# Hybrid attention and gating block: where the splits of the branch weights stand beside z, and where the last raw gate rows lie

## The chip, the core and the metric

One core of a Trainium2 chip. The metric is the device time of one execution in microseconds (us), the median of three runs. Engines: PE (TensorE, matrix products), DVE (VectorE), ACT (ScalarE), POOL (GpSimd) and SP (SyncE, which here issues most DMAs). Each takes its own queue of instructions in order and waits on semaphores.

## The reference

A decoder block on 2048 tokens of width 1024, in float32:

```python
h = _rmsnorm(x, norm_pre_mix[layer])
proj = jnp.einsum('bsd,de->bse', h, w_in[layer])   # q, k, v, u, z, two gates
y_attn = _mixer_dilated_attention(q, k, v)
y_gmlp = _mixer_chunked_gmlp(u, z, ...)
merged = (gate_a * jnp.einsum('bse,ed->bsd', y_attn, w_branch_attn[layer])
          + gate_b * jnp.einsum('bse,ed->bsd', y_gmlp, w_branch_gmlp[layer]))
y = jnp.einsum('bsd,de->bse', merged, w_out[layer])
```

Then a residual, a norm and a squared-ReLU MLP. The attention has three groups of dilated windows; their outputs are combined by a softmax over the groups' log-denominators. u and z go through Gelu, z through a layer norm and a product along the sequence.

## The kernel before

Every float32 matrix product is made of three products of rounded parts: each operand is split into a high part (`hi`, rounded) and the rest (`lo`, a subtraction), and PE runs hi x hi, hi x lo and lo x hi, lines 95 to 97. The helper `split` (line 67) writes the high part on ACT (line 70) or POOL (line 72) and subtracts on DVE or POOL (line 78). `split_in` (line 87) loads a raw row by an SP DMA (line 91) and splits it.

The sequence is cut into four chunks of 512 tokens. Work stands in a generator, `filler` (line 758), which is advanced in steps by other parts of the program: `u`, `z` of chunks 2 and 3, the gate products of `gates` (line 662), and last z of chunks 0 and 1. PE's order is the order in which the program writes it; the order on DVE, ACT, POOL and SP is made by a scheduler, where nothing else is said. `behind()` (line 175) ties what is written under it behind the latest instruction written for each engine, so that the scheduler puts it no earlier.

**Gates.** The gate and u columns are made by seven products each (a scheme of sums of blocks). `seq` lists them with half, operation i and pair n; `LAST` is the place in `seq` of the last ten products. `piece(t)` (line 613) loads the raw weights of product t by an SP DMA (line 627) into a small row `r` of a ring, `split_piece(t)` (line 630) splits it on POOL into one of the `spots`; `PIECES = 4` and `SPLITS = 3` say how many products ahead. The rows are four rows `gr` in two tiles, then `ga11`, `ga9`, `ga10` and two of the tiles that hold results (`zs[8:]`, called ga7 and ga8). Results go to DRAM by SP (line 714) one product later, and one or two entries of `ins` (the loads of the weights of z, `w_z`, and of the activations, `hT_b`) follow each product (line 717).

**z of chunks 0 and 1.** Each chunk has four tiles of 128 tokens; a tile is eight steps of three products (line 95 to 97), so 64 steps. After a tile ACT makes Gelu (line 572) and DVE statistics (lines 574 and 575); after four tiles DVE normalizes (line 579). The raw activations of chunk 1 (`hT_b`, line 1077) are loaded in the first eight steps.

**The combination of attention** (`combine`, line 953) for one chunk is a generator of five pieces: three loads of the groups' outputs into `cw` (line 958); maxima, differences, exponential, normalizers (lines 961 to 974); scaling on ACT (line 979, sixteen small instructions) and DVE (line 982, two); two additions (lines 984 and 985); eight transposes on PE (line 990) whose results ACT copies (line 993) and stores (line 994). Two chunks (2 and 3) are combined during the gates with tiles of their own. Chunks 0 and 1 use one place `cw`, one after the other, during z. The dictionary `todo` (line 1073) says behind which step of z a piece is written (2 stands for chunk 0, 3 for chunk 1):

```python
    todo = {12: (2,), 14: (2,), 17: (2,), 24: (2, 3), 38: (3,), 40: (3,), 43: (3,), 52: (3,)}
    for n in range(1, 54):
        steps(1)
```

**The branch weights** are six rows wb0 to wb5. `load_wb` (line 1063) loads a row into one of two raw rows and splits it, the high part on POOL, the rest on DVE; it is called at every sixth step. Its DMA, its copy on POOL and its subtraction on DVE are placed by the scheduler.

Behind z stands the merge: six rows `yt` are loaded (line 91, from `load_y`) and split on POOL, the gates are loaded (lines 1129 and 1138), opened by a sigmoid on ACT (line 1147), and the products with `wb` and `yt` are multiplied with them on DVE (line 1164).

Of the kernel before, what the change touches and what calls it, by code (L numbers as in the profile page):

```python
# [8 lines left out]
F32 = mybir.dt.float32  # L9
# [7 lines left out]
P = 128  # L17
S = 2048
D = 1024
# [22 lines left out]
def block_kernel(ctx, tc, a, out):  # L42
# [44 lines left out]
    def split_in(w, src, raw=None, hi_eng="pool", lo_eng="dve"):  # L87

        if raw is None:
            raw = f32(w)[:, 1]  # L90
        sp.dma_start(raw, src)
        split(w[:, 0], w[:, 1], raw, hi_eng, lo_eng)
# [82 lines left out]
    def behind():  # L175

        es, t = ExitStack(), mybir.EngineType
        for e in (t.Activation, t.DVE, t.Pool, t.SP):
            es.enter_context(tc.issue_after(next(i for i in reversed(nc.cur_bb.bb.instructions) if i.engine == e)))
        return es  # L180
# [432 lines left out]
    def piece(t):  # L613

        if t >= len(seq):
            return
        half, i, n = seq[t]
        raws = g_["raws"]
        r = raws[t % 4] if t < 8 else raws[4 + (t - LAST - 4) % 5] if t >= LAST + 4 else raws[(t - 8) % 5]
        if i < 3:  # L620
            src = w_src(w_at(n), i - 1)[:, :, :P]
        elif i == 5:
            src = s1g_d[n]
        else:
            kk, m = {6: (0, 0), 7: (0, 1), 3: (1, 0), 4: (1, 1)}[i]
            src = sg_d[n][:, kk, :, m * P:(m + 1) * P]
        sp.dma_start(r.rearrange("p (k c) -> p k c", k=4), src)
        g_["raw"][t] = r
# [33 lines left out]
    def gates():  # L662

        bank, todo, out_, ins = {}, [], [], []
        slots = [None, hp.tile([P, 2, 2, 4, 512], F32R, name="opB", tag="hT", bufs=2)]
        zs = wp.tile([P, 8, 512], F32, name="gz", tag="w", bufs=3)
        zs = [zs[:, n] for n in range(8)]
        xs = [st.tile([P, 512], F32, name=f"gx{n}", tag="ev", bufs=3) for n in range(3)]
        g_["b"].update({(1, 1): hT[2][:, :, :4], (1, 2): hT[2][:, :, 4:]})
        phases = [(half, ops) for half in (1, 0) for ops in PHASES]  # L670
        starts, t = {}, 0
        for n, (half, ops) in enumerate(phases):
            starts[t] = n
            t += PAIRS[half] * len(ops)
        for t, (half, i, n) in enumerate(seq):
            if t in starts:
                ph, t0 = starts[t], t
                if ph + 1 < len(phases):
                    s = (ph + 1) % 2
                    if not slots[s]:  # L680
                        slots[s] = hp.tile([P, 2, 2, 4, 512], F32R, name="opA", tag="hT", bufs=2)
                    for j, i2 in enumerate(phases[ph + 1][1]):
                        new = operand(phases[ph + 1][0], i2, slots[s][:, j])
                        ins += new[0]
                        todo += new[1]
                else:
                    ws, hs = want(5), reload_h(0)
                    ins += ws[:2] + hs[:4] + ws[2:] + hs[4:]
            elif todo and (t - t0) % 3 == 1 and t > t0 + 1:
                w, k = todo.pop(0)  # L690
                with behind():
                    split(w[:, 0, k:k + 2], w[:, 1, k:k + 2], f32(w)[:, 1, k:k + 2], "act", "pool")
            piece(t + PIECES)
            split_piece(t + SPLITS)
            if i in (1, 6, 5, 4):
                bank[n] = psum_mm(f"g{half}{i}{n}")
            p, w, h = bank[n], g_["w"].pop(t), g_["b"][half, i]
            for k in range(4):
                for m, (l, r) in enumerate(((0, 0), (0, 1), (1, 0))):
                    pe.matmul(p, w[:, l, k], h[:, r, k], start=i in (1, 6, 5, 4) and not k and not m,  # L700
                              stop=k == 3 and m == 2, skip_group_check=True)
                if (t, k) == (3, 2) and late:
                    sz_out(*late.pop(0))
                yield
            if t == 3:
                a = [ga.tile([P, 512], F32, name=f"ga{n_}", tag=f"ga{n_}", bufs=1) for n_ in range(12)]
                xs += a[:7]
                zs += a[7:9]
                vs = a[9:11]
                g_["vs"] = vs + xs[8:] + zs[8:]  # L710
                g_["raws"] += a[11:] + vs + zs[8:]
            x, z, fn = xs[n], zs[n], AF.Copy if n < 8 else AF.Gelu_apprx_tanh
            while out_:
                sp.dma_start(*out_.pop())
            for _ in range(2 if half and i == 4 or t in (LAST + 1, LAST + 2) else 1):
                if ins:
                    sp.dma_start(*ins.pop(0))
            if i == 1:
                act.activation(x, p, AF.Copy)
            elif i == 2:  # L720
                act.activation(z, p, fn)
                o = z, 0, 0
            elif i == 6:
                dve.tensor_add(z, x, p)
            elif i == 7:
                dve.tensor_add(x, x, p)
            elif i == 5:
                if (half, n) == (0, 0):
                    g_["vs"] = a[9:11]
                v = g_["vs"].pop(0)  # L730
                g_["vs"].append(v)
                dve.tensor_add(v, x, p)
                o = v, 1, 1
            elif i == 3:
                dve.tensor_add(z, z, p)
                o = z, 0, 1
            else:
                dve.tensor_add(x, x, p)
                o = x, 1, 0
            if n > 7 and i in (5, 3, 4):  # L740
                act.activation(o[0], o[0], fn)
            if i in (2, 5, 3, 4):
                c, dst = 2 * half + o[2], gate_d if n < 8 else u_d
                out_.append((dst[n % 8 * 2 + o[1], :, c * 512:(c + 1) * 512], o[0]))
        sp.dma_start(*out_.pop())
        yield
# [312 lines left out]
    e2r = ExitStack()  # L1059
    wbp = stack(e2r, "wbp", 1, side="right")  # L1060
    wb = [wbp.tile([P, 2, D], F32R, name=f"wb{k}") for k in range(6)]

    def load_wb(k):
        raw = wp.tile([P, D], F32, name=f"wbraw{k}", tag="raw", bufs=2)
        split_in(wb[k], a["w_branch"][:, k, :], raw)

    ez = ExitStack()
    zps[0] = stack(ez, "zp0", 1, side="right")
# [1 line left out]
    next(sg)  # L1070
    while not cw:
        steps(1)
    todo = {12: (2,), 14: (2,), 17: (2,), 24: (2, 3), 38: (3,), 40: (3,), 43: (3,), 52: (3,)}
    for n in range(1, 54):
        steps(1)
        if zin:
            sp.dma_start(*zin.pop(0))
        if n % 6 == 0 and n <= 36:
            load_wb(n // 6 - 1)
        if n == 48:  # L1080
            next(sg)
        for k in todo.get(n, ()):
            combined((0, k))
# [969 lines left out]
```

## Time and profile before

| | us |
|---|---|
| Median of three runs | 2675.07 (2674.3 to 2677.39) |
| The profiled execution, its time | 2677.99 |
| The profiled execution, its span | 2676.0 |
| PE busy | 2617.2 (98%) |
| DVE busy | 1652.9 (62%) |
| POOL busy | 1197.9 (45%) |
| ACT busy | 1087.0 (41%) |

The span goes from the first to the last instruction of the program on the core; the time holds what lies around it, 1.99 us here. The mean granted clock of PE is 0.993. Times inside the trace are counted from the span's start. In rows of a timeline stand the start, the length, the engine, the line, the operation, what is written <- what is read, sizes and count, and in brackets the idle time of the engine before it and who ended it. Buffer numbers are left out of names, so wb0 to wb5 all read wb. "yt" names both the combination's transposes on line 990 and the merge's rows on lines 72 and 78.

### The profile page before, as it was taken

Reading aid. Unit: us, or ns where it says so; the run is one execution under the profiler, and the core shown is the slowest. Engines: PE = TensorE matmul, PEld = TensorE weight load, DVE = VectorE, ACT = ScalarE, POOL = GpSimd, SP = SyncE. Lnnn points to the kernel's source line nnn. Section 1 sums busy time; section 2 is a strip of 40 time slices with the busy share of each in tenths; the row PEclk is TensorE's granted clock in tenths of the full one; section 3 lists DMA queues with packets and bytes.
Section 4 is the critical chain, followed back from the end, with each engine's and each line's share of the span. In section 5 each row is a group of like instructions: output and inputs, shape, how many; then the busy total and the mean of one; then the engine's idle time right before and its main releaser. Section 6 shows DMA issues by size and latency. Waiting matters only on the chain. (4 is left out here: it accounts for less than half of the span.)

```text
span 2676.0 us, 35501 instructions
## 1 busy us (share of the span) xinstructions
PE 2617.2 (98%) x12458; PEld 2185.3 (82%) x12458; DVE 1652.9 (62%) x2793; ACT 1087.0 (41%) x2278; POOL 1197.9 (45%) x1089
## 2 busy tenths in 40 slices
PE   9999999999999996999999999999999999999998
PEld 8888888888888884788878888888888888888887
DVE  5676665535434453765677655655437888888866
ACT  5213111254455432444445555655545333233334
POOL 0363354274464662310233564223315776676645
PEclk9999999999999998999999999999999999999999
DMA  8779768888888898543667464654343212222235
GB/s 320 280 248 319 261 229 292 291 281 251 291 281 243 236 303 301 203 168 134 200 231 262 130 218 159 209 154 129 106 145 119 87 56 87 87 87 87 87 109 214
DMA packets 389284, 528.29 MB, mean 197 GB/s; under 512 B 57009, under 2 KB 242097, under 8 KB 387570
## 3 DMA queue, kind: packets, MB, share of 16 engines
q1 hardware_dynamic: 300336, 436.03, 49.6%
q0 software_dynamic: 14992, 51.65, 5.1%
q10 hardware_dynamic: 73778, 38.35, 4.7%
q8 instruction: 98, 1.61, 0.3%
q14 instruction: 80, 0.66, 0.1%
HBM read 342.77 MB, written 183.17 MB: 197 GB/s over the span
## 5 line engine op out<-in xcount | busy, mean ns | idle before, releaser
L1904 PE MATMUL ya<-T_spots,s 128*128 128x512 f32 x1176 | 289.3, 389 | 1.0 <-ACT T_spots L70 0.6
L70 ACT ACTIVATE s<-sraw 128x768 fp32r<-128x768 f32 (+1 forms) x184 | 127.2, 696 | 330.3 <-POOL sraw L1705 156.2
L1904 PEld LDWEIGHTS ya<-T_spots,s 128*128 128x128 f32 x1176 | 220.6, 188 | 47.6 <-ACT T_spots L70 0.9
L78 DVE TENSOR_TENSOR s<-sraw,s 128x512 fp32r<-128x512 f32 x172 | 184.5, 1097 | 8.5 <-ACT s L70 7.2
L1377 PE MATMUL aa<-B,A 128*128 128x512 f32 x768 | 182.4, 390 | 1.4 <-ACT xs L1391 0.7
L1348 POOL TENSOR_TENSOR s<-w1r 128x512 f32<-128x512 f32 x32 | 42.4, 1324 | 307.7 <-DVE S L78 261.0
L700 PE MATMUL g<-opA,spots 128*128 128x512 f32 x672 | 170.0, 397 | 0.0
L1377 PEld LDWEIGHTS aa<-B,A 128*128 128x128 f32 x768 | 143.9, 188 | 31.9 <-ACT xs L1391 1.1
L700 PE MATMUL g<-opB,spots 128*128 128x512 f32 x648 | 164.5, 398 | 1.3 <-POOL spots L72 0.7
L1904 PE MATMUL yc<-T_spots,s 128*128 128x512 f32 x624 | 159.6, 389 | 0.0
L95 PE MATMUL x<-hT_a,wq 128*128 128x512 f32 x384 | 149.7, 390 | 0.0
L97 PE MATMUL x<-hT_a,wq 128*128 128x512 f32 x384 | 149.4, 389 | 0.0
L96 PE MATMUL x<-hT_a,wq 128*128 128x512 f32 x384 | 149.4, 389 | 0.0
L700 PEld LDWEIGHTS g<-opA,spots 128*128 128x128 f32 x672 | 121.2, 188 | 21.8
L78 POOL TENSOR_TENSOR spots<-gr,spots 128x512 fp32r<-128x512 f32 x98 | 127.7, 1307 | 22.3 <-PE g L700 8.3
L1904 PEld LDWEIGHTS yc<-T_spots,s 128*128 128x128 f32 x624 | 117.2, 188 | 24.3
L700 PEld LDWEIGHTS g<-opB,spots 128*128 128x128 f32 x648 | 116.7, 188 | 23.1 <-POOL spots L72 1.1
L70 ACT ACTIVATE hl<-r 128x512 fp32r<-128x512 f32 x48 | 30.4, 633 | 236.4 <-POOL r L321 89.0
L72 POOL TENSOR_SCALAR spots<-gr 128x512 fp32r<-128x512 f32 x86 | 54.7, 636 | 139.9 <-PE g L700 104.0
L949 DVE TENSOR_REDUCE o<-po 128x256 f32<-128x512 f32 x48 | 33.2, 691 | 133.6 <-PE po L948 133.6
L1704 POOL TENSOR_TENSOR sraw<-sraw 128x256 f32<-128x256 f32 x56 | 42.0, 749 | 161.7 <-DVE s L78 158.4
L78 POOL TENSOR_TENSOR T_spots<-w2r,T_spots 128x512 fp32r<-128x512 f32 x70 | 104.4, 1520 | 7.3 <-ACT T_spots L70 7.3
(422 smaller groups left out, 6960.0 us busy)
## 6 DMA issues: line engine op xcount, KB each, us to landing
w1r<-in_w_mlp_in_dram SPq DMA_DIRECT2D x64, 512.0 KB, 3.8
sraw<-sd SPq DMA_DIRECT2D x128, 256.0 KB, 3.2
qk<-hl SPq DMA_DIRECT2D x24, 1024.0 KB, 5.5
qq<-qk SPq DMA_DIRECT2D x96, 256.0 KB, 5.2
w2r<-in_w_mlp_out_dram SPq DMA_DIRECT2D x16, 1024.0 KB, 7.9
sd<-u ACTq DMA_DIRECT2D x63, 256.0 KB, 3.7
g<-gated SPq DMA_DIRECT2D x58, 256.0 KB, 3.9
gr<-sgd SPq DMA_DIRECT2D x53, 256.0 KB, 4.6
```

The costliest lines, as they stand in the source:

```text
L70: act.activation(hi, src, AF.Copy)
L72: pool.tensor_scalar(hi, src, 1.0, 1.0, op0=OP.mult, op1=OP.mult)
L78: (pool if lo_eng == "pool" else dve).tensor_sub(lo, src, f32(hi))
L95: pe.matmul(ps, lh, rh, start=start, stop=False)
L96: pe.matmul(ps, lh, rl, start=False, stop=False)
L97: pe.matmul(ps, ll, rh, start=False, stop=stop)
L700: pe.matmul(p, w[:, l, k], h[:, r, k], start=i in (1, 6, 5, 4) and not k and not m, stop=k == 3 and m == 2, skip_group_check=True)
L949: dve.tensor_reduce(ot[:, :, j * 64:(j + 1) * 64], po.rearrange("p (b h e) -> p b e h", b=4, h=2), axis=AX.X, op=OP.add)
L1348: pool.tensor_add(s1, a21, a22)
L1377: pe.matmul(p, w[:, l, k, :], h[:, r, k, :], start=i in (1, 6, 5) and not k and not n, stop=k == 3 and n == 2, skip_group_check=True)
L1704: pool.tensor_add(a22, a21, a22)
L1904: pe.matmul(p, s[:, l], w[r], start=i in (1, 2, 5) and not m and not o, stop=m == 1 and o == 2, skip_group_check=True)
```

## The change

In `piece`, `gates` and the loop over z:

```diff
-        r = raws[t % 4] if t < 8 else raws[4 + (t - LAST - 4) % 5] if t >= LAST + 4 else raws[(t - 8) % 5]
+        r = raws[t % 4] if t < 8 else g_["ends"].pop(0) if t >= LAST + 4 else raws[(t - 8) % 5]
...
-            piece(t + PIECES)
+            if t == LAST:
+                g_["ends"] = g_["vs"] + zs[8:]
+            for n_ in (t + PIECES,) if t < LAST else {0: (4, 5), 1: (6, 7), 2: (8,), 3: (9,)}.get(t - LAST, ()):
+                piece(n_ if t < LAST else LAST + n_)
...
-                g_["raws"] += a[11:] + vs + zs[8:]
+                g_["raws"] += a[11:]
...
-            for _ in range(2 if half and i == 4 or t in (LAST + 1, LAST + 2) else 1):
+            for _ in range(2 if half and i == 4 or t in (LAST + 5, LAST + 6) else 1):
...
+    wb_raw = {}
 
     def load_wb(k):
-        raw = wp.tile([P, D], F32, name=f"wbraw{k}", tag="raw", bufs=2)
-        split_in(wb[k], a["w_branch"][:, k, :], raw)
+        wb_raw[k] = wp.tile([P, D], F32, name=f"wbraw{k}", tag="raw", bufs=2)
+        sp.dma_start(wb_raw[k], a["w_branch"][:, k, :])
+
+    def split_wb(k):
+        with behind():
+            split(wb[k][:, 0], wb[k][:, 1], wb_raw.pop(k), "pool", "dve")
...
-    todo = {12: (2,), 14: (2,), 17: (2,), 24: (2, 3), 38: (3,), 40: (3,), 43: (3,), 52: (3,)}
-    for n in range(1, 54):
+    todo = {14: (2,), 16: (2,), 18: (2,), 28: (2, 3), 40: (3,), 42: (3,), 45: (3,), 54: (3,)}
+    for n in range(1, 56):
...
-        if n % 6 == 0 and n <= 36:
-            load_wb(n // 6 - 1)
+        if n in (20, 24, 30, 34, 44, 50):
+            split_wb((20, 24, 30, 34, 44, 50).index(n))
+        if n in (6, 9, 20, 24, 30, 34):
+            load_wb((6, 9, 20, 24, 30, 34).index(n))
```

The load and the split of a branch row are separate now; the split is tied behind a step of z (20, 24, 30, 34, 44, 50). The combination's pieces stand two to four steps later. The last six raw gate rows (products LAST+4 to LAST+9) go one each into six rows: ga9, ga10, cv0 and cv1 (`vs`) and ga7 and ga8, and their loads are written in the first four of the last ten products. The doubled entries of `ins` come four products later. No instruction of arithmetic is added or taken away. The line numbers of the changed kernel are higher by 3 from line 694 on and by more behind the loops of z.

The scheduler's order on DVE at the end of chunk 0's combination in the kernel before (cw_9554 is the place of both combinations, E_0 belongs to chunk 0, M_1 to chunk 1, wb3 to wb5 are branch rows):

```order
L982 TENSOR_TENSOR cw_9554<-cw_9554,E_0_9625 128x4x256
L78 TENSOR_TENSOR wb3_9535<-wbraw3_9710,wb3_9535 128x1024
L982 TENSOR_TENSOR cw_9554<-cw_9554,E_0_9625 128x4x256
L78 TENSOR_TENSOR wb4_9536<-wbraw4_9751,wb4_9536 128x1024
L984 TENSOR_TENSOR cw_9554<-cw_9554 128x4x256
L985 TENSOR_TENSOR cw_9554<-cw_9554 128x4x256
L78 TENSOR_TENSOR wb5_9537<-wbraw5_9794,wb5_9537 128x1024
L961 TENSOR_TENSOR M_1_9804<-cw_9554 128x16
```

The same place on DVE in the changed kernel (bs_02 and bs_03 are statistics of the third and fourth tile of chunk 0):

```order
L985 TENSOR_TENSOR cw_9554<-cw_9554,E_0_9627 128x4x256 x2
L987 TENSOR_TENSOR cw_9554<-cw_9554 128x4x256
L988 TENSOR_TENSOR cw_9554<-cw_9554 128x4x256
L574 BN_STATS bs_02_9699<-z_0_9559 128x6
L575 BN_AGGR mv_0_9560<-bs_02_9699 128x2
L78 TENSOR_TENSOR wb0_9532<-wbraw0_9589,wb0_9532 128x1024
L574 BN_STATS bs_03_9755<-z_0_9559 128x6
L575 BN_AGGR mv_0_9560<-bs_03_9755 128x2
```

In the kernel before wb0 to wb4 stand ahead of the last additions of chunk 0's combination; now the first of them, wb0, stands behind its end, and the third tile's statistics with it.

DVE at the end of chunk 1's combination, before:

```order
L974 TENSOR_TENSOR E_1_9807<-E_1_9807,M_1_9804 128x4x4 x3
L575 BN_AGGR mv_1_9777<-bs_10_9826 128x2
L982 TENSOR_TENSOR cw_9554<-cw_9554,E_1_9807 128x4x256 x2
L984 TENSOR_TENSOR cw_9554<-cw_9554 128x4x256
L539 SCALAR_TENSOR_TENSOR bsp0_9542<-rowsum0_9882,lngb0_9543,bsp0_9542 128x128
L985 TENSOR_TENSOR cw_9554<-cw_9554 128x4x256
```

and in the changed kernel:

```order
L977 TENSOR_TENSOR E_1_9814<-E_1_9814,M_1_9811 128x4x4 x3
L985 TENSOR_TENSOR cw_9554<-cw_9554,E_1_9814 128x4x256
L78 TENSOR_TENSOR wb5_9537<-wbraw5_9786,wb5_9537 128x1024
L985 TENSOR_TENSOR cw_9554<-cw_9554,E_1_9814 128x4x256
L78 TENSOR_TENSOR wb4_9536<-wbraw4_9749,wb4_9536 128x1024
L987 TENSOR_TENSOR cw_9554<-cw_9554 128x4x256
L988 TENSOR_TENSOR cw_9554<-cw_9554 128x4x256
```

Two subtractions of branch rows now stand between the steps of chunk 1's combination; wb1, wb2 and wb3 stand ahead of it, between the normalization of chunk 0 and the statistics of chunk 1.

SP behind the loads of `ur`, with the semaphores that each entry waits for (DMAHW are the landings of earlier DMAs). Before:

```order
L91 DMA wbraw3_9710<-in_w_branch_dram 128x1024 [waits DMAHW0_49,DVE_49]
L91 DMA wbraw4_9751<-in_w_branch_dram 128x1024 [waits DMAHW6_49,DMAHW1_49,DVE_49]
L91 DMA wbraw5_9794<-in_w_branch_dram 128x1024 [waits DMAHW7_49,DMAHW5_49,DVE_49]
L958 DMA cw_9554<-att2_76 128x4x264 [waits DVE_49]
L958 DMA cw_9554<-att1_75 128x4x264 [waits DVE_49]
L958 DMA cw_9554<-att0_74 128x4x264 [waits DMAHW3_49,PE_49]
L91 DMA yt20_10000<-yad_77 128x512 [waits DMAHW7_49,PE_49]
```

and in the changed kernel:

```order
L1069 DMA wbraw3_9708<-in_w_branch_dram 128x1024 [waits DMAHW7_49,DMAHW2_49,DVE_49]
L961 DMA cw_9554<-att0_74 128x4x264 [waits DMAHW0_49,PE_49]
L961 DMA cw_9554<-att1_75 128x4x264 [waits DMAHW1_49]
L961 DMA cw_9554<-att2_76 128x4x264
L1069 DMA wbraw4_9749<-in_w_branch_dram 128x1024 [waits DMAHW3_49,DVE_49]
L1069 DMA wbraw5_9786<-in_w_branch_dram 128x1024 [waits DMAHW7_49,DMAHW4_49,DVE_49]
L91 DMA yt20_10000<-yad_77 128x512 [waits PE_49]
```

Chunk 1's three loads into cw come ahead of the loads of wb4 and wb5, and all three stand behind PE's transposes of chunk 0. As a raw row is one of two, wb3's load waits until DVE has subtracted wb1, wb4's for wb2 and wb5's for wb3, before as now.

## The prediction

> **What bounds the kernel now.** TensorE (PE) is busy 98% of the span, so only time in which it stands or runs at a lower clock can be won. I read its waits first, over the whole span.
>
> ```profile
> PE yt L990 <- issue: 27.2, 2, 23.0
> ...
> PE z L97 <- DMA hT_b<-hbd: 1.2, 1, 1.2
> ...
> PE g L700 <- POOL spots L72: 0.7, 1, 0.7
> PE g L700 <- POOL spots L78: 0.6, 1, 0.6
> ```
>
> One place dominates: the transposes (L990) that end the combination of chunks 0 and 1, two waits. Then the table of busy time by stretch, cut at those waits (columns: stretch, length, busy time of PE, PE's weight loads, DVE, ACT and POOL with counts, granted clock, DMA share, GB/s).
>
> ```profile
> 1033.70:1057.09 23.39, 0.40 (x3) 0.03 (x1) 15.72 (x26) 5.81 (x19) 7.72 (x6) 0.61 0.70 247
> 1057.09:1080.70 23.61, 23.61 (x94) 18.98 (x94) 15.37 (x32) 12.49 (x27) 11.39 (x11) 0.88 0.48 153
> 1080.70:1084.90 4.20, 0.00 (x1) 0.04 (x1) 4.20 (x4) 0.00 (x0) 3.01 (x2) 0.77 0.00 0
> 1084.90:1095.67 10.77, 10.77 (x42) 9.02 (x43) 2.21 (x7) 1.79 (x3) 0.00 (x0) 0.77 0.28 99
> ```
>
> Each wait is followed by work at a lower granted clock: (1 - 0.88) x 23.61 = 2.8 us and (1 - 0.77) x 10.77 = 2.5 us more. The two waits cost 23.0 + 2.8 + 4.2 + 2.5 = 32.5 us; the small ones named above 2.5 us. Nothing else here can be won.
>
> Why the first wait: the timelines of DVE, POOL and SP.
>
> ```profile
> 1049.54 1.23 DVE L78 TENSOR_TENSOR wb<-wbraw,wb 128x1024 fp32r<-128x1024 f32 x1 [0.94 <-POOL wb L72]
> 1050.68 2.06 DVE L982 TENSOR_TENSOR cw<-cw,E 128x1024 f32<-128x1024 f32 x1
> ...
> 1055.11 1.87 DVE L985 TENSOR_TENSOR cw<-cw 128x1024 f32<-128x1024 f32 x1
> ```
>
> ```profile
> 1037.49 1.05 POOL L72 TENSOR_SCALAR wb<-wbraw 128x1024 fp32r<-128x1024 f32 x1 [10.86 <-DMA wbraw<-in_w_branch_dram]
> ```
>
> DVE takes its queue in order. The first combination's data lay ready, but the subtractions of the branch weights (L78) stood ahead of and between its steps, and the first of them could not run before wb0's raw row had landed, at 1037.4. The last step, L985, ended at 1056.98; PE started at 1057.09.
>
> **The change, part by part.** Four edits.
>
> *1. The subtractions leave the first combination.* It now needs its third load, issued by SP at 1023.33, then the chain below (SP issue; landing times of these loads; DVE; ACT; the last step undisturbed, in the same work on tile A).
>
> ```profile
> 1023.33 0.43 SPq L958 DMA_DIRECT2D cw<-att  x1
> ```
>
> ```profile
> DMA to landing us min/median/max: 3.7/5.6/7.2
> ```
>
> ```profile
> 1046.10 0.33 DVE L969 TENSOR_TENSOR Z<-E,cw 128x16 f32<-128x16 f32 x3
> ...
> 1047.38 1.22 DVE L982 TENSOR_TENSOR cw<-cw,E 128x1024 f32<-128x1024 f32 x1
> ```
>
> ```profile
> 1047.43 3.93 ACT L979 ACTIVATE cw<-cw,E 128x64 f32<-128x64 f32 x16 [2.12 <-DVE E L974]
> ```
>
> ```profile
> L982 DVE TENSOR_TENSOR A<-A,E x4: 1218/1221/1224, 974.5 to 994.5; 128x1024 f32<-128x1024 f32 x4
> ...
> L985 DVE TENSOR_TENSOR A<-A x2: 1216/1286/1355, 979.7 to 997.9; 128x1024 f32<-128x1024 f32 x2
> ```
>
> Landing 1023.3 + 5.6 = 1028.9; about 1.6 for the maxima, differences and exponential: 1030.5; L969 to L982 takes 1.28: 1031.8; ACT's sixteen scalings 3.93: 1035.7; L985 1.29: 1037.0. The transposes also move from step 24 to step 28 of z. A step of z is three matmuls:
>
> ```profile
> 1033.26 0.39 PE L95 MATMUL z<-w_z,hT_b 128*128 128x512 f32 x1
> 1033.49 0.39 PE L96 MATMUL z<-w_z,hT_b 128*128 128x512 f32 x1
> ```
>
> Start to start 0.23 us, so 0.68 a step; PE gets there at 1057.09 - 23.0 + 4 x 0.68 = 1036.8. So about 0.5 us of wait is left of 23.0, drains included (0 to 2, as the load lands in 3.7 to 7.2), too short for the clock. Minus 23.0 and minus 2.8, plus 0.5.
>
> *2. The second combination.* Its transposes go from step 52 to 54. With the first wait gone PE gets there at 1080.7 - 23.4 - 2.8 + 1.4 + 0.5 = 1056.4. What does DVE have to do before? Its queue now runs: fourth tile's statistics, L579, wb1, L579, wb2, two L579, statistics, wb3, statistics and row sums, maxima of chunk 1, L982, wb5, L982, wb4, L984, L985. And wb3's load stands in SP's queue behind wb1's subtraction, and chunk 1's loads behind wb3's load.
>
> ```profile
> 1065.55 0.60 ACT L572 ACTIVATE z<-z 128x512 f32<-128x512 f32 x1 [4.02 <-PE z L97]
> 1066.17 1.28 ACT L102 ACT_TABLE_LOAD   x1
> 1067.46 0.30 ACT L102 ACTIVATE r_ln<-mv,edge 128x4 f32<-128x4 f32 x1
> ```
>
> ```profile
> 1068.80 3.50 DVE L579 TENSOR_SCALAR z<-z,mv,r_ln 128x512 f32<-128x512 f32 x4
> ```
>
> ```profile
> L72 POOL TENSOR_SCALAR wb<-wbraw x6: 1046/1154/1939, 1037.5 to 1054.7; 128x1024 fp32r<-128x1024 f32 x6
> L78 DVE TENSOR_TENSOR wb<-wbraw,wb x6: 1211/1218/1226, 1038.6 to 1056.9; 128x1024 fp32r<-128x1024 f32 x6
> ...
> DMA to landing us min/median/max: 3.8/4.0/10.2
> ```
>
> ```profile
> L574 DVE BATCH_NORM_STATS2 bs<-z 128x6 f32<-128x512 f32 x8 | 5.5, 685 | 26.1 <-ACT z L572 26.1
> ...
> L539 DVE SCALAR_TENSOR_TENSOR bsp<-rowsum,lngb,bsp 128x128 f32<-128x128 f32 x4 | 1.2, 330 | 0.0
> ```
>
> PE ends the fourth tile at 1037.1 + 0.8 (transposes) + 3 x 0.68 = 1039.9; Gelu at 1040.3; L579 follows Gelu by 1068.80 - 1065.55 = 3.25: 1043.55. One L579 (0.87) and wb1 (1.22): 1045.6. Now SP may load wb3: 4.0, POOL's copy 1.05, landing and copy done at 1050.7; wb3: 1052.0. Statistics and row sums, 0.69 + 0.18 + 4 x 0.33 and a first maximum 0.17: 1054.4. Chunk 1's three loads, issued within some 1.5 us behind wb3's load, have landed by then even at 7.2 (1054.3). Differences, exponential and L969 to L982: 0.35 + 0.3 + 1.3 = 2.0: 1056.4. Already PE stands. L982: 1057.6; wb5, whose raw row was issued behind wb3 (1052.0) and is copied at 1057.8: 1059.0; L982, wb4, L984, L985: 1.22 + 1.22 + 1.22 + 1.29 = 5.0: **1064.0**, if nothing disturbs DVE.
>
> POOL does. It copies wb2 beside L579 and wb4 beside the small steps, and from 1058 it splits the six yt rows, beside the end of this chain. The rows of before show what that costs.
>
> ```profile
> 1077.22 3.16 DVE L982 TENSOR_TENSOR cw<-cw,E 128x1024 f32<-128x1024 f32 x2
> 1080.41 2.17 DVE L984 TENSOR_TENSOR cw<-cw 128x1024 f32<-128x1024 f32 x1
> ...
> 1082.77 2.02 DVE L985 TENSOR_TENSOR cw<-cw 128x1024 f32<-128x1024 f32 x1
> ```
>
> ```profile
> 1074.61 2.56 POOL L78 TENSOR_TENSOR yt<-yt 128x512 fp32r<-128x512 f32 x2
> 1079.28 4.44 POOL L78 TENSOR_TENSOR yt<-yt 128x512 fp32r<-128x512 f32 x2
> ```
>
> ```profile
> L78 POOL TENSOR_TENSOR yt<-yt 128x512 fp32r<-128x512 f32 x6 | 9.7, 1625 | 0.2
> ...
> L72 POOL TENSOR_SCALAR yt<-yt 128x512 fp32r<-128x512 f32 x6 | 4.9, 826 | 13.2 <-DMA yt<-yad 13.2
> ```
>
> L984 takes 0.95 more, L985 0.73, an L982 0.36 to 0.84: with 0.9 for each of two copies the end is at most 1064.0 + 1.8 + 0.4 + 0.95 + 0.73, about 1068. I take **1067**, near the disturbed rows, since the same splits lie beside the same steps. Wait of PE: 1067 - 1056.4 = 10.6, where it was 4.2 (bounds 7.6 and 11.6). The slow clock behind it stays at 2.5.
>
> A page of the Trainium skill speaks against the change here. "SBUF — State Buffer", section "SBUF: two separate sides", says that a DVE instruction with two SBUF inputs and a GpSimd instruction that reads SBUF exclude each other for a whole instruction. The rows above bear out a block, but not one for each instruction: L982 twice took 3.16, not 2.44 plus two subtractions of POOL. By the rule alone the gain below would be about 13.5 (a rival, below).
>
> A second rule concerns the first combination: "ScalarE: Activation LUTs", section "What ACT_TABLE_LOAD costs", gives 1.28 for the load and 1.38 more for a drain. Here the load takes 1.28 and the next instruction starts 0.01 behind it, so the trace does not show the drain; by the page the first combination would end 1.1 later and the gain would be 1.1 less.
>
> *3. The last raw rows have places of their own,* so their loads come sooner and the two waits for POOL's spots (1.3 us) should go. But the first tile of z then waits for hT_b:
>
> ```profile
> 1013.74 0.32 SPq L717 DMA_DIRECT2D hT_b<-hbd  x1
> ```
>
> ```profile
> 990.00:1020.00 30.00, 28.70 (x128) 22.70 (x126) 12.68 (x21) 7.58 (x21) 10.39 (x10) 1.00 1.03 389
> ```
>
> ```profile
> gated<-ga SPq DMA_DIRECT2D x5, 256.0 KB, 8.2
> ```
>
> The DMA engines are full from 990 to 1020 (share 1.03), and the same bytes stand ahead of the last hT_b load; that two of the w_z and hT_b loads are issued some steps later only shortens a queue that is long enough (8.2 us to land 256 KB). PE would wait 1.3 longer for hT_b: 0 in the sum, bounds a gain of 2.5 (both kinds of wait gone) and a loss of 1.5.
>
> *4. What follows.* The yt loads stand behind wb5's in SP's queue, the yt splits behind wb5's copy on POOL: 1058 + 9.7 + 4.9 = 1072.6. PE begins the merge at 1067 + 10.77 - 1.36 = 1076.4, so PE's wait covers them; were that wait gone, PE would reach the merge at about 1063.3 and wait there for yt, up to 9 us. The first gate rows wait, as before, for the landing of the second combination's stores and keep their place to PE. Behind that the order is the same, and I put it at 0.
>
> Sum: 23.0 + 2.8 + 4.2 - 0.5 - 10.6 = **18.9 us** off. The profiled execution has a span of 2676.0 and a time of 2677.99; it would be 2659.1. The median of the runs is 2675.07, 2.9 lower, and is what I subtract from: **2656**.
>
> **The rivals.** *No wait is left* (0.08): all 32.5 go but 0.5, 2643. It needs L985's end by 1056.4; the order speaks against it, since wb3's load, copy and subtraction alone hold DVE until 1052.0. By edit 4 the yt splits would take up to 9 of it back.
>
> *Each DVE step waits for a whole POOL step* (0.12): from wb5 on five steps, each with one subtraction of POOL (2.56 / 2) ahead: 1060 + 6.2 + 6.4 = 1072.6, wait 16.2, 13.4 off, 2661.7. For it: 4.44 for two yt subtractions. Against it: 3.16 for two L982.
>
> *SP's queue stalls at the end of the gates* (0.06), slower. Four raw rows are now loaded into rows whose store to DRAM must have landed, and w_z and hT_b stand behind them. If SP stood a whole landing (8.2) for each, 4 x 8.2 = 32.8, the last hT_b and all behind it came that much later: 32.8 - 18.9 = 13.9 slower, 2689. It turns slower by over 5.4 when hT_b's last load is issued over 24 us after 1013.74. Against it: in the new order each such load stands five to seven entries behind its store, so the landing runs while other entries are issued.
>
> *The wait only moves* (0.06): L985 of chunk 1 ends after 1080.7, because its loads or wb3's land as late as 10.2 and DVE is held at each step; within 5.4 of 2675.
>
> **Numbers.** The forecast has 0.68; its own range, from L985's end at 1064.0 (21.9 off) to 1068 (17.9 off) with 1.5 for the spread of the three runs, is 2652 to 2659. Upwards the range takes in the POOL rival, 2661.7, with 1.5 of the first combination's bound and the 1.5 of the runs: 2665. Downwards it takes in edit 3's 2.5 and the first combination's 0.5: 2653.2 - 3.0 - 1.5, about 2648. Left out are the first, third and fourth rivals, 0.20. A measurement tells 0.2% (5.4 us) from nothing: faster 0.88, same 0.06, slower 0.06.
>
> **What would show it.** Right: PE waits at L990 once for under 2 us and once for 8 to 12; L985 of chunk 1 ends 30 us after the first Gelu of z's fourth tile at the latest; wb3's copy on POOL starts about 4 us after wb1's subtraction; the waits for spots are gone and that for hT_b is longer by as much; no new wait of PE at the first merge products. Wrong: a wait of over 2 us at the first transposes (then the loads of chunk 0 are late), a wait at b's products for yt or gates, or z beginning later than 1015.

## The result, and the profile after

Two sets of runs stand beside each other: before 2676.23 us (median of 4 runs, 2674.3 to 2681.6), after 2659.64 us (median of 4, 2658.39 to 2661.19). The ratio is 0.9935, with a 95% interval of 0.9918 to 0.9952. In two later sets of runs the changed kernel came to 0.9943 (0.9929 to 0.9957) and 0.9935 (0.9921 to 0.9948). The profiled execution of the changed kernel has a time of 2661.19 and a span of 2659.4; its span is 16.6 us shorter than that of before. One of the five executions of e6 below ran at a granted clock of 0.751 and took 3272.83 us; e6's median and ratio are of the other four.

PE's waits over the whole span of the changed kernel:

```profile
PE yt L993 <- issue: 11.5, 1, 11.5
PE b L95 <- DVE g L1174: 5.3, 4, 2.2
...
PE z L97 <- DMA hT_b<-hbd: 1.8, 2, 1.1
...
PE z L95 <- DMA hT_b<-hbd: 0.7, 1, 0.7
```

Line 990 is line 993 now. Two waits of 23.0 and 4.2 have become one of 11.5. No row for spots is left. The wait for hT_b has grown from 1.2 to 2.5, in three pieces, and b's wait for DVE's products with the gates from 1.8 in two places to 5.3 in four. PE's timeline shows the places:

```profile
1014.92 0.50 PE L97 MATMUL z<-w_z,hT_b 128*128 128x512 f32 x1 [1.14 <-DMA hT_b<-hbd]
...
1016.78 0.80 PE L95 MATMUL z<-w_z,hT_b 128*128 128x512 f32 x1 [0.66 <-DMA hT_b<-hbd]
...
1018.67 0.80 PE L97 MATMUL z<-w_z,hT_b 128*128 128x512 f32 x1 [0.67 <-DMA hT_b<-hbd]
...
1036.43 1.06 PE L993 MATMUL yt<-ident,cw 128*128 128x128 f32 x8
...
1067.64 1.94 PE L993 MATMUL yt<-ident,cw 128*128 128x128 f32 x8 [11.53 <-issue]
```

The first transposes stand without a wait between the products of z. The products behind the second and third wait for hT_b take 0.80 us, where one takes 0.39 at full clock. The table by stretch (columns as in the prediction) shows that clock:

```profile
1010.43:1015.43 5.00, 3.86 (x17) 2.83 (x16) 0.69 (x1) 0.63 (x1) 0.00 (x0) 1.00 1.03 412
1015.43:1020.43 5.00, 3.68 (x9) 2.18 (x9) 0.00 (x0) 0.00 (x0) 0.00 (x0) 0.62 1.05 392
1020.43:1025.43 5.00, 5.00 (x17) 3.91 (x17) 0.95 (x3) 0.60 (x1) 1.02 (x4) 0.69 0.83 224
1067.64:1076.44 8.80, 8.80 (x36) 7.47 (x36) 0.88 (x2) 3.08 (x4) 5.93 (x6) 0.79 0.33 121
```

At z's start the granted clock is 0.62 and 0.69 for ten microseconds, from the second of the three waits on: (0.38 + 0.31) x 5 = 3.45 us by the slices. These count idle time too; by the products, which start 0.43 us apart instead of 0.23, about 2.7 are lost. Before, the clock there was 1.00. Behind the second transposes it is 0.79 over 8.80 us, 1.85 lost.

DVE's last step of chunk 0's combination, and its chain ahead of the second transposes:

```profile
1035.11 1.22 DVE L988 TENSOR_TENSOR cw<-cw 128x1024 f32<-128x1024 f32 x1
...
1043.32 1.22 DVE L78 TENSOR_TENSOR wb<-wbraw,wb 128x1024 fp32r<-128x1024 f32 x1
...
1049.93 1.22 DVE L78 TENSOR_TENSOR wb<-wbraw,wb 128x1024 fp32r<-128x1024 f32 x1 [1.34 <-POOL wb L72]
...
1053.27 0.17 DVE L965 TENSOR_TENSOR M<-M,cw 128x16 f32<-128x16 f32 x1
...
1054.64 0.91 DVE L974 TENSOR_TENSOR M<-M,Z 128x16 f32<-128x16 f32 x1
...
1055.87 1.48 DVE L977 TENSOR_TENSOR E<-E,M 128x16 f32<-128x16 f32 x3
1057.27 1.21 DVE L985 TENSOR_TENSOR cw<-cw,E 128x1024 f32<-128x1024 f32 x1
1058.41 2.28 DVE L78 TENSOR_TENSOR wb<-wbraw,wb 128x1024 fp32r<-128x1024 f32 x1
1060.61 1.62 DVE L985 TENSOR_TENSOR cw<-cw,E 128x1024 f32<-128x1024 f32 x1
1062.16 2.28 DVE L78 TENSOR_TENSOR wb<-wbraw,wb 128x1024 fp32r<-128x1024 f32 x1
1064.36 1.62 DVE L987 TENSOR_TENSOR cw<-cw 128x1024 f32<-128x1024 f32 x1
1066.09 1.44 DVE L988 TENSOR_TENSOR cw<-cw 128x1024 f32<-128x1024 f32 x1
```

Behind L988 of chunk 0 these are wb1, wb3 (which waits for its raw row's copy), chunk 1's last maximum, two small steps, and then the end of the combination with wb5 and wb4 among its steps; the last step ends at 1067.53. From 1057.27 to 1067.53 it takes 10.26 us. L974 and L977 took 0.17 and 0.35 in chunk 0; here POOL copies wb4 and wb5 beside them. Behind that it splits yt:

```profile
1054.47 1.05 POOL L72 TENSOR_SCALAR wb<-wbraw 128x1024 fp32r<-128x1024 f32 x1 [4.57 <-DMA wbraw<-in_w_branch_dram]
1055.69 1.04 POOL L72 TENSOR_SCALAR wb<-wbraw 128x1024 fp32r<-128x1024 f32 x1 [0.17 <-DMA wbraw<-in_w_branch_dram]
...
1057.41 2.20 POOL L78 TENSOR_TENSOR yt<-yt 128x512 fp32r<-128x512 f32 x1
1059.58 1.59 POOL L72 TENSOR_SCALAR yt<-yt 128x512 fp32r<-128x512 f32 x1
1061.25 2.11 POOL L78 TENSOR_TENSOR yt<-yt 128x512 fp32r<-128x512 f32 x1
1063.33 3.13 POOL L72 TENSOR_SCALAR yt<-yt 128x512 fp32r<-128x512 f32 x2
1066.43 3.46 POOL L78 TENSOR_TENSOR yt<-yt 128x512 fp32r<-128x512 f32 x2
1069.86 1.20 POOL L72 TENSOR_SCALAR yt<-yt 128x512 fp32r<-128x512 f32 x2
1071.02 2.55 POOL L78 TENSOR_TENSOR yt<-yt 128x512 fp32r<-128x512 f32 x2
```

Once DVE is done, two subtractions take 2.55 and two copies 1.20; beside DVE one subtraction takes 2.1 to 2.2 and one copy 1.6.

**Three stretches.** Single executions of one kernel differ by several microseconds (2657.5 to 2664.9 in 15 runs of the changed kernel), and not at the place of the change: in the traces the first gate product that reads `opB` starts anywhere from 575.7 to 583.1, with the same program text ahead of it. So the traces are compared by stretch, from this product on ("first gate product" below): A from it to z's first product, B from there to the merge's first product, C from there to the end of the span (each from the starts of these products on PE's timeline). The fourth column is the granted clock in the first 15 us of B, the fifth PE's waits for hT_b.

| kernel | A | B | C | clock | hT_b |
|---|---|---|---|---|---|
| before | 436.2 | 80.5 | 1580.3 | 1.00 | 1.2 |
| changed | 434.4 | 66.0 | 1583.0 | 0.77 | 2.5 |
| changed, e4 | 436.0 | 65.2 | 1582.1 | 0.89 | 2.9 |
| changed, e11 | 434.4 | 65.8 | 1582.0 | 0.89 | 3.0 |
| gate part alone, e2 | 434.4 | 80.7 | 1580.4 | 1.00 | 2.5 |
| z part alone, e1 | 435.4 | 63.1 | 1580.4 | 1.00 | 1.5 |
| z part alone, e10 | 435.2 | 63.0 | 1580.6 | 1.00 | 1.1 |
| late wb4, wb5, e3 | 434.4 | 61.1 | 1582.0 | 0.89 | 1.9 |
| yt on ACT, e5 | 434.5 | 64.7 | 1585.3 | 0.89 | 2.5 |
| `ins` as before, e6 | 434.5 | 64.5 | 1579.6 | 1.00 | 3.6 |
| late, loads, row sums, e7 | 434.5 | 58.5 | 1581.0 | 0.89 | 3.0 |
| the same, old gate part, e8 | 435.6 | 55.8 | 1581.3 | 1.00 | 1.2 |
| places alone, e9 | 442.1 | 61.5 | 1579.0 | 1.00 | 0 |

Of the 16.6 us of the two profiled spans 3.0 lie ahead of the first gate product, 1.8 in A and 14.5 in B; C gives 2.6 back. C ranges from 1579.0 to 1583.0 over all traces but e5, where PE waits in the merge for yt. It is 1580.3 to 1580.6 in before, e1, e2 and e10 and 1582.0 to 1583.0 in the changed kernel's three; e6 and e9, which differ from the changed kernel only around the last gates, have 1579.6 and 1579.0. Whether the kernel has a part in that can't be told from so few traces. The waits in C come and go from trace to trace.

### The profile page after: what moved, and what is told of

Read it like the earlier page. It is cut to its first block, busy times and chain, and to the rows that moved or that the text cites. A ratio compares the mean times of both kernels' runs of the same rounds, so it can differ in the third digit from the quotient of the medians.

```text
span 2659.4 us, 35499 instructions
## 1 busy us (share of the span) xinstructions
PE 2617.5 (98%) x12458; PEld 2185.1 (82%) x12458; DVE 1649.7 (62%) x2793; ACT 1087.4 (41%) x2279; POOL 1201.2 (45%) x1089
```

## The experiments

**Theories.** A: the whole gain comes from the two combinations, and what is left of the wait is the length of DVE's queue ahead of L988. B: the gate rows carry part of it. C: POOL's work beside DVE sets the length of that queue's end. E, F, G: three reasons for the longer wait for hT_b.

**e1 and e10, the z part alone.** The gate part is as before:

```diff
-        r = raws[t % 4] if t < 8 else g_["ends"].pop(0) if t >= LAST + 4 else raws[(t - 8) % 5]
+        r = raws[t % 4] if t < 8 else raws[4 + (t - LAST - 4) % 5] if t >= LAST + 4 else raws[(t - 8) % 5]
...
-            for n_ in (t + PIECES,) if t < LAST else {0: (4, 5), 1: (6, 7), 2: (8,), 3: (9,)}.get(t - LAST, ()):
-                piece(n_ if t < LAST else LAST + n_)
+            piece(t + PIECES)
...
-                g_["raws"] += a[11:]
+                g_["raws"] += a[11:] + vs + zs[8:]
...
-            for _ in range(2 if half and i == 4 or t in (LAST + 5, LAST + 6) else 1):
+            for _ in range(2 if half and i == 4 or t in (LAST + 1, LAST + 2) else 1):
```

> The changed kernel with the gate part as it was before (old places of the last raw gate rows, old order of their loads), so that only the splits of the branch rows and the combination's pieces have moved. Theory A (the whole gain comes from the two combinations beside z; the gate rows give nothing): time within 1.5 us of the changed kernel's 2659.6, ratio to before 0.993 to 0.9945; the two waits for spots are back (about 1.3 us) and the wait for hT_b at z's first tile is back at about 1.2 instead of 2.5. Theory B (the gate rows carry part of the gain): 2661 to 2663, ratio 0.9945 to 0.9955, because the spots waits are back and the hT_b wait stays.

Measured: 2658.3 us (median of 6), ratio 0.9933 (0.9920 to 0.9946). Its waits:

```profile
PE yt L990 <- issue: 11.6, 1, 11.6
...
PE z L97 <- DMA hT_b<-hbd: 1.2, 1, 1.2
...
PE g L700 <- POOL spots L78: 0.6, 1, 0.6
```

The gain is there in full without the gate part, as theory A has it. B is 63.1, shorter than the changed kernel's 65.2 to 66.0.

**e2, the gate part alone** (the kernel before with those same lines changed).

> The kernel before with the gate part alone changed (the last six raw gate rows in places of their own). Theory A: no difference, 2676 +- 1.5, ratio 0.9995 to 1.0005: the spots waits (1.3 us) go and the wait for hT_b grows from 1.2 to about 2.5; the waits of 23.0 and 4.2 at the transposes stay, together 27 +- 1. Theory B: 1 to 2.5 us faster, ratio 0.999 or less.

Measured: 2676.89 us (median of 12), ratio 1.0003 (0.9992 to 1.0013).

```profile
PE yt L993 <- issue: 27.4, 2, 23.0
...
PE z L97 <- DMA hT_b<-hbd: 1.9, 2, 1.2
```

No difference. The waits at the transposes stay (27.4), those for spots go, those for hT_b grow to 2.5 (0.6 of it on line 95); here the clock stays at 1.00 behind them. Theory B falls.

**e3, wb4 and wb5 behind the combination.**

```diff
-        if n in (20, 24, 30, 34, 44, 50):
-            split_wb((20, 24, 30, 34, 44, 50).index(n))
+        for k in {20: (0,), 24: (1,), 30: (2,), 34: (3,), 46: (4, 5)}.get(n, ()):
+            split_wb(k)
```

> The changed kernel with the splits of wb4 and wb5 written behind the additions of chunk 1's combination instead of among them. Theory A (DVE's queue ahead of L988 sets PE's wait of 11.5 us): L988 ends two subtractions of 2.28 us earlier, at about 1063.0; the wait at the second transposes is about 7.0 instead of 11.5 and the time is 4.5 us less than the changed kernel's, about 2655; no wait at the merge's first products, since POOL's yt splits (end 1073.6) still lie ahead of the use of the last yt row (about 1076). Theory C (POOL's yt splits hold each step of DVE, whatever stands between): the remaining steps only stretch into the freed time, L988 ends at 1065 or later and the gain is 2.3 or less.

Measured: 2655.57 us (median of 6), ratio 0.9925 (0.9911 to 0.9939); the wait at the transposes is 8.7. DVE's end of the combination:

```profile
1057.64 3.83 DVE L985 TENSOR_TENSOR cw<-cw,E 128x1024 f32<-128x1024 f32 x2
1061.51 2.17 DVE L987 TENSOR_TENSOR cw<-cw 128x1024 f32<-128x1024 f32 x1
1063.78 1.44 DVE L988 TENSOR_TENSOR cw<-cw 128x1024 f32<-128x1024 f32 x1
```

The two subtractions are gone from the chain, 4.56 us of it, and it is shorter by only 2.7 (7.58 where it was 10.26); the wait fell by 2.8. The steps that remain took up the rest: two L985 took 3.83 where chunk 0's took 2.48, L987 2.17 for 1.62. So in the trace the gain is the subtractions' own time (2 x 1.14, start to start, in e5 below) and little more, between A's 4.5 and C's 2.3, nearer to C; L988 ends at 1065.2, as C has it. The medians of e3 and e4, the changed kernel beside it, differ by 5.8, but their runs overlap (2652.6 to 2660.1 and 2658.0 to 2664.9).

**e5, no split of yt on POOL beside the chain.**

```diff
-    yt = load_y(2, ("pool", "pool"))
+    yt = load_y(2, ("act", "pool"))
```

> The changed kernel with the high parts of the six yt rows of the first merge made on ACT instead of POOL. In ACT's order they stand behind the Gelu of z's last tile, so POOL subtracts nothing for yt beside the end of chunk 1's combination. It is a measurement of that end, not a faster kernel. Theory C (POOL's work stretches DVE's steps): from the first L985 of chunk 1 to the end of L988 it takes about 7.0 us instead of 10.26, the subtractions of wb5 and wb4 take 1.22 instead of 2.28 and L987 1.23 instead of 1.62; PE's wait at the transposes is about 8.3 instead of 11.5. Rival (DMA writes or ACT's scalings stretch them): still about 10.3 us and a wait of 11.5. In both cases the merge then waits 4 to 8 us for yt and the time is 0 to 5 us over the changed kernel's.

Measured: 2669.42 us, one run. The wait at the transposes is 8.1. DVE:

```profile
1063.05 1.22 DVE L985 TENSOR_TENSOR cw<-cw,E 128x1024 f32<-128x1024 f32 x1
1064.19 1.22 DVE L78 TENSOR_TENSOR wb<-wbraw,wb 128x1024 fp32r<-128x1024 f32 x1
1065.33 1.22 DVE L985 TENSOR_TENSOR cw<-cw,E 128x1024 f32<-128x1024 f32 x1
1066.46 1.22 DVE L78 TENSOR_TENSOR wb<-wbraw,wb 128x1024 fp32r<-128x1024 f32 x1
1067.60 1.22 DVE L987 TENSOR_TENSOR cw<-cw 128x1024 f32<-128x1024 f32 x1
1068.92 1.22 DVE L988 TENSOR_TENSOR cw<-cw 128x1024 f32<-128x1024 f32 x1
```

The same six instructions in the same order take 7.09 us where they took 10.26, each 1.22. Theory C is shown for this place: POOL's splits cost the chain 3.2 us. ACT's scalings stand beside the chain as before (3.93 us), so they aren't what stretched it. The time is not better, as was foreseen, since PE then waits 2.9 for ACT's and 1.8 for POOL's parts of yt at the merge; it is higher than expected mainly because this execution came to its first gate product at 583.1, 7.1 later than the first trace of the changed kernel.

**e4 and e11, the changed kernel again.**

> The changed kernel once more, on the chip of the other three. Time 2659.6 +- 1.5. Its profile tells what the 2.6 us are by which the stretch from the merge's first product to the end was longer (1582.96 us against 1580.33 before). Theory A (landing times of single loads differ from execution to execution): other waits at the merge's products than 1.8, 2.2 and 1.4 us, and a stretch anywhere from 1580 to 1583.5. Theory D (the earlier start of the merge finds its loads less far): the same waits at the same products and 1583 +- 0.3.

> The changed kernel, for comparison with e9 and e10 on one chip: 2659.6 to 2661.4 +- 1.5, waits for hT_b of 2.5 to 2.9 us in three places, and a slow clock (a slice under 0.95) in z's first 15 us.

Measured: 2661.41 (6 runs) and 2659.88 us (5 runs). The wait at the transposes is 11.4 and 12.0, that for hT_b 2.9 and 3.0 in three places, and each time the clock falls there (0.89 over 15 us; 0.77 in the first trace). At the merge the waits differ: in e4 b waits 2.3 in two places, in e11 4.3 in four, and a wait of 1.4 of the MLP's products for DVE's line 1412 in the first trace is there in e4 (1.1) and not in e11. C is 1582.1 and 1582.0. Theory D falls; the signs of theory A are there, though that landing times are the cause is not shown.

**e6, the loads of w_z and hT_b where they stood.**

```diff
-            for _ in range(2 if half and i == 4 or t in (LAST + 5, LAST + 6) else 1):
+            for _ in range(2 if half and i == 4 or t in (LAST + 1, LAST + 2) else 1):
```

> The changed kernel with the two doubled entries of the loads of w_z and hT_b back at the products where they stood before (second and third of the last ten) and the raw gate rows in their new places. Theory E (these later loads split z's wait for hT_b in three, and the split wait brings the half clock behind it): the waits for hT_b add up to 1.5 us or less in at most two places, no slice of z's first 15 us has a granted clock under 0.95, from z's first product to the merge's first product it takes 62.5 to 63.5 us (66.0 and 65.2 in the two traces of the changed kernel), and the time is 1 to 3 us less than the changed kernel's. Rival F (the six raw rows, issued together, push hT_b back in full DMA engines): the waits for hT_b stay at 2.5 in three places and the stretch at 65 or more.

Measured: 2659.97 us (median of 4), ratio 0.9940 (0.9927 to 0.9954), as the changed kernel.

```profile
PE z L97 <- DMA hT_b<-hbd: 2.4, 2, 1.2
...
PE z L95 <- DMA hT_b<-hbd: 1.2, 2, 0.7
```

The waits are longer still, 3.6 in four places, and the clock stays at 1.00. Theory E falls on both counts: the later `ins` aren't the reason, and a longer wait need not bring the slow clock. Rival F is half met: the waits are there, its stretch of 65 or more is not (B is 64.5).

**e9, the places alone,** with the raw rows' loads at the old products.

```diff
-            for n_ in (t + PIECES,) if t < LAST else {0: (4, 5), 1: (6, 7), 2: (8,), 3: (9,)}.get(t - LAST, ()):
-                piece(n_ if t < LAST else LAST + n_)
+            piece(t + PIECES)
...
-            for _ in range(2 if half and i == 4 or t in (LAST + 5, LAST + 6) else 1):
+            for _ in range(2 if half and i == 4 or t in (LAST + 1, LAST + 2) else 1):
```

> The changed kernel with the last six raw gate rows in their own places, but their loads and the loads of w_z and hT_b written at the products where they stood before the change (one product's raw row at a time). Theory G (the wait for hT_b grows because the raw rows' loads are issued earlier, ahead of hT_b in full DMA engines): the waits for hT_b fall back to 1.2 to 1.5 us in one or two places without a slow clock behind them, the waits for spots stay away or under 0.7, the stretch from z's first product to the merge's first product is 62.5 to 63.5 us (63.1 with the old gate part, 64.5 to 66.0 with the new one), and the time is 1 to 3 us less than the changed kernel's. Rival (the places themselves, or chance, decide): waits for hT_b of 2.5 or more, as in the changed kernel.

Measured: 2656.79 us (median of 5), ratio 0.9933 (0.9921 to 0.9946), which is not to be told from e10 (2661.2, 0.9938 with 0.9926 to 0.9951) or e11 beside it. PE waits nowhere for hT_b, but theory G is not shown by that. z starts 442.1 us after the first gate product, 6 to 8 later than in the other traces, and the last load of hT_b (issued at 1016.39, 7.6 to landing) lands 446.7 after it. In the four traces with the old gate part it lands at 441.5 to 442.4, in the eight with the new places and the early loads at 441.6 to 444.1. So hT_b did not land sooner here; PE came later. POOL is late again, and now the slow clock stands ahead of z (the last row is from before):

```profile
1014.09 0.73 PE L702 MATMUL g<-opB,spots 128*128 128x512 f32 x2 [0.89 <-POOL spots L72]
1015.45 4.14 PE L702 MATMUL g<-opB,spots 128*128 128x512 f32 x10 [0.63 <-POOL spots L78]
...
1012.77 2.56 PE L700 MATMUL g<-opB,spots 128*128 128x512 f32 x10 [0.63 <-POOL spots L78]
```

Ten products in 4.14 us took 2.56 before. A holds 2.4 of another wait (one of the attention's products, which lie among the gates, for a load); without it A + B is 501.2, the changed kernel's 500.4. Theory G had expected 1 to 3 us less time than the changed kernel's and got 3.1 between medians whose runs overlap, so how much the early issue adds to the wait for hT_b stays open.

> The kernel of e1 (old gate part, new z part) once more beside the changed kernel, so that the gate part's worth is read from twice as many runs. If the gate part costs time (1.3 us more waiting for hT_b and the slow clock behind it, against 1.1 us of waits for spots): 1 to 3 us below e11. If the gate part is worth 0, as the prediction had it: within 1 us of e11.

Over both sets the z part alone has a median of 2659.4 (11 runs) and the changed kernel over three sets one of 2659.85 (15 runs): as whole executions tell it, the gate part is worth 0 within their spread. The two sets disagree in sign: e1 is 3.1 below e4 beside it, e10 1.3 above e11, outside both bands of its expectation.

**e7 and e8, three more moves.** e3 with

```diff
-        if n in (6, 9, 20, 24, 30, 34):
-            load_wb((6, 9, 20, 24, 30, 34).index(n))
-        if n == 48:
+        if n in (6, 9, 20, 29, 31, 34):
+            load_wb((6, 9, 20, 29, 31, 34).index(n))
+        if n == 54:
             next(sg)
```

and e8 the same with the old gate part.

> Experiment e3 with two more moves: chunk 1's three loads are written ahead of the loads of wb3 and wb4, and the row sums of the spatial weights (PE's L537 and DVE's L539) move from step 48 to step 54. Theory A (the chain wb3's load, chunk 1's loads, row sums, combination sets the wait): chunk 1's maxima run at about 1049 instead of 1053.7, L988 ends at 1057 to 1058.5 instead of 1065.1, PE's wait at the transposes is 1 to 2.5 instead of 8.7, and POOL's yt splits are next: PE waits 2 to 4 us at the first products of the merge for the last yt rows. Time 2648 to 2652. Rival C (POOL's copies and splits hold DVE's steps wherever they stand): L988 ends at 1060 or later, wait 4 or more, time 2652 to 2655.

> The kernel of e7 with the gate part as it was before the change. If the gate part costs time by the clock behind the waits for hT_b (theory E): 1 to 3 us less than e7, with one or two waits for hT_b, no slow clock at z's start, and a wait for spots of 0.6 to 1.3 back. If the gate part does nothing: the same as e7 within 1 us.

Measured: e7 2654.35 us (median of 5), ratio 0.9918 (0.9904 to 0.9931); e8 2653.6 us (median of 4), ratio 0.9915 (0.9901 to 0.9928). Every run of e7 (2651.4 to 2654.5) is faster than the fastest of the changed kernel's 15 (2657.5), though the intervals of the ratios overlap. The wait is 5.1 in both, not 1 to 2.5. DVE and ACT of e7 tell why:

```profile
1047.83 0.17 DVE L965 TENSOR_TENSOR M<-M,cw 128x16 f32<-128x16 f32 x1
1048.03 0.35 DVE L968 TENSOR_TENSOR E<-cw,M 128x16 f32<-128x16 f32 x3
...
1051.80 0.35 DVE L972 TENSOR_TENSOR Z<-E,cw 128x16 f32<-128x16 f32 x3 [0.65 <-ACT E L969]
...
1058.37 1.79 DVE L988 TENSOR_TENSOR cw<-cw 128x1024 f32<-128x1024 f32 x1
```

```profile
1049.62 0.60 ACT L572 ACTIVATE z<-z 128x512 f32<-128x512 f32 x1 [4.84 <-PE z L97]
1050.23 1.28 ACT L969 ACT_TABLE_LOAD   x1
1051.53 0.24 ACT L969 ACTIVATE E<-E 128x48 f32<-128x48 f32 x1
```

Chunk 1's maxima run at 1047.8, 5.4 earlier than in the changed kernel, as expected. But the exponential stands in ACT's queue behind the Gelu of z's next tile, which could not start before PE's end at 1049.6: the differences are ready at 1048.4 and the table load starts at 1050.2, 1.8 us later. Between there and L988's end at 1060.2 stand wb3 (1.1), three row sums (0.8) and 0.6 that L988 loses to POOL's copy of wb5. Together that is 4.3 of the 5.1. The wait, the end and the time are those of rival C, but POOL's share in them is only the 0.6, so C's numbers came by other causes. At the merge PE waits 0.5 for POOL's yt, not 2 to 4. e8's B is 2.7 shorter than e7's and its A 1.1 longer; the medians differ by 0.75.

## Why the prediction was right, and where its sizes were off

2656 was forecast, 2659.64 came; the sign and the stated range (2648 to 2665) held, while the forecast's own range (2652 to 2659) was missed by 0.6. The gain is 16.6 us between the medians of one set, where 18.9 was forecast. On the profiled executions 2659.1 was forecast, 2661.19 came, and there 3.0 of the gain lie ahead of the first gate product, which the change does not touch: that is luck.

*Edit 1 was right.* The first combination needs no DVE work ahead of it but its own: the wait of 23.0 and the 2.8 of slow clock are gone, and the 0.5 that was left over is 0. L988 of chunk 0 ended at 1036.33 (1037.0 forecast) and PE came at 1036.43 (1036.8). The drain of 1.38 that the prediction weighs is not seen: the table load in this chain ends at 1029.48 and the exponential starts at 1029.60.

*Edit 2 was right in mechanism.* The chain was forecast step by step, and the trace follows it: wb1's end 1045.6 forecast, 1044.54 measured; wb3's end 1052.0 and 1051.15; the first L985 (line 982 before) 1056.4 and 1057.27; the end 1067 and 1067.53; PE there at 1056.4 and 1056.11. The wait is 11.5 (11.4 and 12.0 in the repetitions) for 10.6. That the end agrees to 0.5 us is partly luck. POOL cost 5.0 us where 3.0 was taken (3.9 at most). Its copies of wb4 and wb5 held L974 and L977 for 1.87 more than in chunk 0, as the 0.9 for each of two copies has it. Its splits of yt then added 3.2 (e5), where 2.1 was allowed, and most of that went not to L984 and L985 but to the branch subtractions (2.28 for 1.22 each). Against that wb3 ended 0.85 earlier than forecast, and the undisturbed end takes 7.1 (e5) where 7.6 was counted. The clock behind these transposes cost 1.85, where 2.5 was put; by the same sum it is 1.4 to 3.1 over the traces with one long wait.

*The rival that each DVE step waits for a whole POOL step* (wait 16.2) was wrong in the count, not in kind. In the 10.26 us POOL works off not five subtractions but two and the beginning of a third. A subtraction alone takes 2.55 / 2 = 1.27; DVE's own 7.09, two of those and the 0.22 that L988 loses to the third are 9.9. The Trainium skill's page "SBUF — State Buffer", section "SBUF: two separate sides", says that the two kinds exclude each other for the whole instruction; for the subtractions the runs agree with it here to 0.4 us. By the same rule the three copies of yt in the chain (1.59 here, 0.60 alone) would hold DVE as well and add 1.8, 11.7 in all, which the chain did not take.

*Edit 3 left out a term:* "PE would wait 1.3 longer for hT_b: 0 in the sum". The exchange itself came as forecast: the waits for spots (1.3) went, that for hT_b grew by 1.3. For the profiled pair that is z's earlier start, as the prediction has it: counted from the first gate product z starts at 434.4 instead of 436.2, and the last load of hT_b lands at 442.7 instead of 442.4. Beside e1 and e10 it is about half of it (z 0.8 to 1.0 earlier, the load 0.8 to 1.1 later). What was left out is the clock. Beside three waits of 1.14, 0.66 and 0.67 within 5 us the granted clock is 0.62 and 0.69, 3.45 us by the slices in the first trace; (1 - 0.89) x 15 = 1.7 us in e3, e4, e5, e7 and e11. The prediction priced the clock behind the two long waits, and not here. In stretch A + B the z part alone saves 18.2 and 18.4 us (516.7 before, 498.5 and 498.3 in e1 and e10), near the forecast 18.9; with the gate part it is 16.3, 15.6 and 16.5. Whole executions do not bear out this difference: the z part alone gains 16.7 and 15.3 between medians, the changed kernel 16.6, 13.6 and 16.6. So the clock's price is read from traces alone. The ledger for the profiled pair: 23.0 + 2.8, then 4.2 - 11.5, then 2.5 - 1.85 for the clock behind the second transposes, then 1.8 in A, - 1.3 for hT_b and - 3.45 for the clock there, in sum 16.2; measured 516.7 - 500.4 = 16.3. With the 2.7 read from the products in place of the 3.45 the sum is 17.0, so the agreement to 0.1 is partly luck.

*Edit 4 was right:* the yt splits end at 1073.57 (1072.6 forecast), the merge starts at 1076.44 (1076.4), and PE does not wait for yt. "Behind that 0" holds within C's own spread of 4 us. That the start of the merge agrees to 0.1 us is partly luck: this execution reached its gates 3.0 us earlier than the one of before.

*What was to show it* came so: no wait at the first transposes, one of 11.5 at the second; L988 ends 27.9 us after the Gelu of z's fourth tile (1039.60); wb3's copy starts at 1048.85, 4.3 after wb1's subtraction; z begins at 1010.43. One sign of being wrong came as well, a wait at b's products for gates: 1.8 us at 1107.30, 31 us into the merge, where it was 0.3 before (1.2 in e4, 1.4 in e11, 0.9 in e1). It is not at the first products, and what brings it was not tested.

Two slips in the sums are small. The 23.4 by which PE comes sooner to the second transposes is the whole stretch, of which PE stood 23.0; with that the wait would have been 10.2. And a wait of 16.2 gives 13.3 off, not 13.4.

Open is what decides on the slow clock. With the new places and the early loads it came in six of eight traces (changed, e3, e4, e5, e7, e11; two or three waits for hT_b, 1.9 to 3.0 us in sum) and not in e2 and e6, where the waits were as long or longer; with the old gate part (before, e1, e8, e10; 1.1 to 1.5 us) it never came there. The Trainium skill's page "TensorE: Matmul & The Clock Gate", section "HAM oscillation — how this bites in real kernels", gives idle gaps over about 3.4 us as what throttles; the trace differs, since no gap here is over 1.22.

## What to carry to other kernels

In an in-order queue, look for work that waits for a late load and stands ahead of a chain that PE waits for; tying it behind that chain's last step was worth nearly the whole wait here, and then the next entry in some queue (POOL's splits, then ACT's exponential) sets the end. A wait of PE that is exchanged for another of the same length need not be free: here a slow clock came with the new one in six of eight traces, so look for it and price it as a risk. A wait that is gone in a trace can also be gone because PE came later (e9): compare when the load landed. And compare kernels by the stretch that the change touches, since single executions differed by as much as 7 us ahead of it, and read the gain from whole executions too.

## What the runs showed of the hardware

- Small DVE instructions are held by POOL too, and by a copy, not only by a subtraction: three of 128x16 (L972) took 0.35 us alone and 1.20 beside POOL's copy of a 128x1024 row (e3, e5). In the changed kernel L974 (0.91 for 0.17) ends at 1055.55 and the copy beside it at 1055.52.
- Taking two instructions out of a chain that POOL disturbs saved little more than their undisturbed time (2.7 of 4.56 us in e3, 2.3 undisturbed): most of the disturbance moved to the instructions that stayed.
- ACT's instruction behind a table load of 1.28 us starts 0.02 us after its end (e7's rows above).
